# Decoder trunk on one core: the merge gates and branch projections with activations as the stationary operand

## The chip, the cores and the metric

The kernel runs on one core of a Trainium2 chip. The metric is the device time of one launch in microseconds. Three runs of the kernel before gave 1503.16, 1503.56 and 1505.4 us; the median is 1503.56 us. A profile of one execution is shown as rows: engines are PE (TensorE matmul), PEld (TensorE weight load), DVE (VectorE), ACT (ScalarE), POOL (GpSimd) and SP (SyncE, which issues nearly all DMAs here).

## The reference

One layer of a decoder trunk for 256 tokens of width 2048. The part around the change:

```python
proj = h @ w_in                       # columns: q, kv, gates, mLSTM inputs, merge_g (2 x 2048)
y_nsa = nsa_attention(...)            # 256 x 1024
y_ml = mlstm(...)                     # 256 x 1024
g_nsa, g_ml = split(sigmoid(merge_g))
merged = g_nsa * (y_nsa @ w_br_nsa) + g_ml * (y_ml @ w_br_ml)     # 256 x 2048
y = merged @ w_o
```

Before it stand a modulated layer norm and the first 5664 columns of the input projection, after it a residual with two layer norms, a gated MLP with a depthwise convolution (w_up, w_down), and a last norm. The modulation vectors (shift, scale, gate, twice) are a matrix-vector product of a conditioning vector with w_ada, 50 MB of weights.

## The kernel before

**Precision and tiles.** A product is made of three fp32r matmuls: each operand is split into a high part and a rest, and high x high, high x rest and rest x high are summed in PSUM. `load_split` (L99 to L111) streams one 512 KB weight tile (128 x 1024) by SP's queue into one of seven `w` buffers, ACT rounds it into `wh` (L109, four buffers) and DVE subtracts to get `wl` (L110, four buffers).

**Which operand stands still.** A matmul loads a 128 x 128 stationary operand and streams up to 512 columns of the other. `mm_b` holds 128 weight columns still and streams 256 tokens (three matmuls of 256 columns); the result has channels on the partitions. `mm_a` holds 128 tokens of the activations still and streams 512 weight columns (three matmuls of 512 columns for each half of the tokens); the result has tokens on the partitions. The down and output projections (`proj_rows`) and the blocks `ps_a` of the input projection use `mm_a`; the merge gates (tile `ps_mg`) and the branch projections (`ps_br`) use `mm_b`.

**Stages.** The input projection runs over four groups of k tiles (`GROUPS` = 3, 4, 5, 4 of 128 rows); each group does 24 blocks `ps_b`, then 6 blocks `ps_a` in two halves. In the last group the mLSTM gates are worked out as well (`gate_steps`: cumulated forget gates, tile `ps_F`; the compressed-attention scores, `ps_sc`; a transposition `ps_uT`; a running maximum by a scan on DVE, L477; the way back, `ps_mc`, L481; its negative `nT4`, L484 and L485). Then comes the attention and mLSTM stage, in an order on PE that is written out by hand: between its short, dependent pieces (`ml_weights` with `ps_w` and `ps_S`, `nsa_probs`, `nsa_out`, `ml_out`) a call `fill(n)` puts n weight tiles of the merge gates, 40 tiles in all. The merge stage does the other merge gates and all branch projections, multiplies, adds and splits the result into `mgT` (channels on the partitions), the operand of the output projection `ps_o`. Outside the stage with the hand-written order, a scheduler sets the order on each engine.

**The second stream.** The w_ada products run on DVE (L182, tile `w` times the row `crow`, one 512 KB tile each, through the same seven `w` buffers). A ticker hands them out at a rate per weight tile: a share worked out from the group sizes in the first three groups, `GR1` in the last, and the three `RATES`: while filling, in the merge stage, in the output projection. What is left by tile 22 of the output projection is put in at once (`tk.drain`).

**PSUM.** Two pools of four banks: `psm` for the big products, `psa` for the rest.

Of the kernel before, what the change touches and what calls it, by code (L numbers as in the profile page):

```python
# [14 lines left out]
P = 128  # L15
# [38 lines left out]
def build(ctx: ExitStack, tc: tile.TileContext, d, out, dbg=None):  # L54
# [280 lines left out]
    gates0 = pg.tile([P, NG0, 512], F32, name="gates0", tag="gates0")  # L335
# [98 lines left out]
    def gate_steps(misc):  # L434
# [3 lines left out]
        nc.scalar.activation(gsig, projA[:, :, A_G:A_G + 24], AF.Sigmoid)  # L438
        nc.scalar.activation(so, so, AF.Sigmoid)
# [6 lines left out]
        nc.vector.tensor_sub(lf, mn, lf)  # L446
        yield
# [51 lines left out]
    for gi, kn in enumerate(GROUPS):  # L499
        nxt = gi < len(GROUPS) - 1  # L500
        if nxt:
            tk.add(ada_mod(k0 + kn, k0 + kn + GROUPS[gi + 1]))
            rate = 4 * GROUPS[gi + 1] / (6 * kn)
        else:
            rate = GR1
# [27 lines left out]
        for c in range(6):  # L533
            pss = [bank(psm, "ps_a%d" % t) for t in range(2)]
            aw = AW if c < 4 else 512
            for k in range(k0, k0 + kn):
                wh, wl = next(wa if c < 4 else wv)
                for t in range(2):
                    mm_a(pss[t][:, :aw], hT, k, t, wh, wl, k == k0, k == k0 + kn - 1)
                if not nxt and c > 2 and (k - k0) % 2:  # L540
                    next(steps, None)
            for t in range(2):
                dst, src = projA[:, t, c * AW:(c + 1) * AW], pss[t][:, :aw]
                if c >= 4:
                    dst = mv1[:, t, 2 * c - 8:2 * c - 6, :MDV]
                    src = src.rearrange("p (h v) -> p h v", v=MDV)
                if gi == 0:
                    nc.scalar.copy(dst, src)
                else:
                    nc.vector.tensor_add(dst, src, dst)  # L550
            if not nxt:
                if c == 2:
                    while comp:
                        work()
                    misc = pa.tile([P, 4, S], F32, name="misc", tag="c4")
                    steps = gate_steps(misc)
                    next(steps)
# [3 lines left out]
    for _ in steps:  # L561
        pass
# [25 lines left out]
    def paired_gen(w, i0, kt, xt, nm):  # L588

        ps = bank(psm, "ps_" + nm)  # L590
        for b in range(2):
            for hf in range(kt):
                wh, wl = load_split(w[i0 + b * kt + hf])
                for k in range(8):
                    mm_b(ps[:, b * S:(b + 1) * S], wh, wl, k, xt[b], hf * 8 + k, hf == 0 and k == 0,
                         hf == kt - 1 and k == 7)
                yield
        yield ps

    def paired(w, i0, kt, xt, rate, nm):  # L600
        for ps in paired_gen(w, i0, kt, xt, nm):
            if ps is None:
                tk.tick(rate)
        return ps

    def merge_pair(j, rate):
        return paired(d["w_mg"], j * 4, 2, (hT, hT), rate, "mg")
# [3 lines left out]
    def fill_gen():  # L611
        for j in range(NG0 + NG1):
            for ps in paired_gen(d["w_mg"], j * 4, 2, (hT, hT), "mg"):
                if ps is None:
                    yield
            if j < NG0:
                nc.scalar.copy(gates0[:, j, :], ps)
            else:
                held[j] = ps
# [175 lines left out]
    with tc.manual_schedule(engines={mybir.EngineType.PE}):  # L795
        fill(F0)
# [26 lines left out]
        fill(4 * (NG0 + NG1))  # L823
# [11 lines left out]
    nc.scalar.activation(gates0, gates0, AF.Sigmoid)  # L835
    for j in MORD:
        if j < NG0:
            gt = gates0[:, j, :]
        else:
            gt = t2([P, 512], "gt")  # L840
            nc.scalar.activation(gt, held.pop(j) if j in held else merge_pair(j, RATES[1]), AF.Sigmoid)
# [102 lines left out]
    def hold_o(c, k, m):  # L944
        if c == 0 and k < KD // 2:
# [5 lines left out]
                     ((4, load_x), (12, lambda: load_ln(lnr, 0)), (22, tk.drain)))  # L951
# [202 lines left out]
def pack(inputs):  # L1154
# [87 lines left out]
```

## Time and profile before

| | us |
|---|---|
| median of 3 runs | 1503.56 |
| the profiled execution | 1502.99 |
| its span, first to last instruction | 1501.1 |
| PE busy | 1447.9 |
| DVE busy | 1104.9 |
| ACT busy | 726.6 |

The stages in that execution, from the span's start: start and input projection to 308 us, attention with filling to 480, merge to 641, output projection to 726, norms to 758, MLP to 1484, last norm to 1501.1. A matmul's row gives its own duration, which is longer than the distance to the next one, since matmuls overlap; the rate is read from the starts, or from a row of the chain that has many of them (its time over its count). The granted clock is a share of 2.4 GHz: 1.00 or 0.50 (1.2 GHz).

### The profile page before, as it was taken

The page shows a single profiled execution, that of the slowest core. Times are in us where ns is not written, and L with a number is a line of the kernel's source. Part 1 is how long each engine was busy: PE and PEld are TensorE (multiplying, and loading weights), DVE is VectorE, ACT ScalarE, POOL GpSimd, SP SyncE. Part 2 cuts the span into 40 slices and gives each one's busy share as a digit, 9 for nine tenths or more (in the row PEclk, how much of TensorE's full clock was granted, in tenths as well). Part 3 has the DMA queues.
Part 4 walks back from the last instruction along what each step waited for, and adds up shares of the span by engine and source line. Part 5 has one row for each costly group of instructions (what it writes and reads, how often), then busy time and mean ns, then how long its engine had stood idle before and what let it go on. Part 6 is the DMA issues. An engine that isn't in the chain of part 4 may idle for free.

```text
span 1501.1 us, 23706 instructions
## 1 busy us (share of the span) xinstructions
PE 1447.9 (96%) x9178; PEld 1298.6 (87%) x9178; DVE 1104.9 (74%) x1669; ACT 726.6 (48%) x1037; POOL 2.1 (0%) x6
## 2 busy tenths in 40 slices
PE   5999999989999999999699999999999999999997
PEld 4989998879889999988688888888898888888887
DVE  7889886777776888778878878865556666665566
ACT  5644343637555444434465554553335555554341
POOL 0000000000000000000000000000000000000000
PEclk7999999989999999999799999999999999999998
DMA  9999897865768999898368868866666666666661
GB/s 360 349 332 360 287 321 277 295 220 171 286 204 274 339 344 340 291 365 321 111 212 279 281 229 285 271 209 196 193 190 195 191 186 191 187 188 190 196 209 59
DMA packets 103792, 374.84 MB, mean 250 GB/s; under 512 B 11648, under 2 KB 11776, under 8 KB 102912
## 3 DMA queue, kind: packets, MB, share of 16 engines
q1 hardware_dynamic: 103680, 373.34, 73.6%
q8 instruction: 72, 1.18, 0.3%
q14 instruction: 40, 0.33, 0.1%
HBM read 371.19 MB, written 2.10 MB: 249 GB/s over the span
## 4 chain that ended last, share of the span: by engine, by line
PE 86%; DVE 8%; DMA 3%; issue 2%; ACT 1%; SPq 0%; DVEq 0%; ACTq 0%
PE ps_up L83 33%; PE ps_d L83 16%; PE ps_mg L83 12%; PE ps_b L83 7%; PE ps_br L83 6%; PE ps_o L83 4%; PE ps_a L83 4%; DVE w L182 2%; DVE wl L110 2%; PE ps_y L83 1%; ACT wh L109 1%; PE ps_s L83 1%; DVE xz L937 1%; DVE xz L932 1%; DMA xt<-in_x_dram 1%
## 5 line engine op out<-in xcount | busy, mean ns | idle before, releaser
L110 DVE TENSOR_TENSOR wl<-w,wh 128x1024 fp32r<-128x1024 f32 (+1 forms) x478 | 575.6, 1206 | 331.9 <-ACT wh L109 328.4
L109 ACT CAST wh<-w 128x1024 fp32r<-128x1024 f32 (+1 forms) x478 | 495.5, 1038 | 659.0 <-PE ps_up L83 150.3
L83 PE MATMUL ps_up<-h2T,wh 128*128 128x512 f32 x1408 | 496.4, 396 | 0.0
L83 PE MATMUL ps_up<-h2T,wl 128*128 128x256 f32 x1408 | 396.2, 282 | 0.0
L83 PEld LDWEIGHTS ps_up<-h2T,wh 128*128 128x128 f32 x1408 | 265.4, 189 | 62.2
L83 PEld LDWEIGHTS ps_up<-h2T,wl 128*128 128x128 f32 x1408 | 264.7, 188 | 0.1
L182 DVE SCALAR_TENSOR_TENSOR w<-w,crow 128x1024 f32<-128x1024 f32 x192 | 232.7, 1217 | 0.0
L83 PE MATMUL ps_d<-wh,uTt 128*128 128x512 f32 (+1 forms) x792 | 210.6, 354 | 0.0
L83 PE MATMUL ps_mg<-hT,wh 128*128 128x256 f32 x1024 | 188.9, 286 | 0.0
L83 PEld LDWEIGHTS ps_mg<-hT,wh 128*128 128x128 f32 x1024 | 158.0, 188 | 7.2 <-issue 7.0
L83 PEld LDWEIGHTS ps_d<-wh,uTt 128*128 128x128 f32 x792 | 140.4, 189 | 20.6
L83 PE MATMUL ps_b<-hT,wh 128*128 128x256 f32 x768 | 138.3, 283 | 5.4 <-ACT wh L109 4.0
L83 PE MATMUL ps_mg<-hT,wl 128*128 128x256 f32 x512 | 143.1, 280 | 0.0
L83 PE MATMUL ps_d<-wl,uTt 128*128 128x512 f32 (+1 forms) x396 | 140.0, 354 | 0.0
L83 PEld LDWEIGHTS ps_b<-hT,wh 128*128 128x128 f32 x768 | 118.6, 191 | 10.3 <-ACT wh L109 4.8
L83 PE MATMUL ps_a<-wh,hT 128*128 128x392 f32 (+1 forms) x384 | 110.6, 364 | 0.0
L83 PE MATMUL ps_b<-hT,wl 128*128 128x256 f32 x384 | 106.7, 282 | 1.3 <-DVE wl L110 1.3
L83 PEld LDWEIGHTS ps_mg<-hT,wl 128*128 128x128 f32 x512 | 96.4, 188 | 0.0
L83 PEld LDWEIGHTS ps_d<-wl,uTt 128*128 128x128 f32 x396 | 74.9, 189 | 10.4
L83 PEld LDWEIGHTS ps_a<-wh,hT 128*128 128x128 f32 x384 | 71.6, 190 | 8.2 <-issue 2.1
L83 PEld LDWEIGHTS ps_b<-hT,wl 128*128 128x128 f32 x384 | 72.6, 190 | 3.0 <-DVE wl L110 2.2
L83 PE MATMUL ps_a<-wl,hT 128*128 128x392 f32 (+1 forms) x192 | 69.5, 362 | 0.0
(248 smaller groups left out, 1390.7 us busy)
## 6 DMA issues: line engine op xcount, KB each, us to landing
w<-in_w_ada_dram SPq DMA_DIRECT2D x192, 512.0 KB, 4.9
w<-in_w_up_dram SPq DMA_DIRECT2D x176, 512.0 KB, 4.4
w<-in_w_down_dram SPq DMA_DIRECT2D x90, 512.0 KB, 4.1
w<-in_w_mg_dram SPq DMA_DIRECT2D x64, 512.0 KB, 5.0
w<-in_w_in_b_dram SPq DMA_DIRECT2D x48, 512.0 KB, 5.3
w<-in_w_br_dram SPq DMA_DIRECT2D x32, 512.0 KB, 5.1
w<-in_w_o_dram SPq DMA_DIRECT2D x32, 512.0 KB, 5.5
w<-in_w_in_a_dram SPq DMA_DIRECT2D x32, 392.0 KB, 4.6
```

What stands on the lines that cost most here:

```text
L83: nc.tensor.matmul(o, lhsT, rhs, start=start, stop=stop)
L109: nc.scalar.copy(wh[:, :n], t[:, :n])
L110: lows.append(nc.vector.tensor_sub(wl[:, :n], t[:, :n], wh[:, :n]))
L182: ins = nc.vector.scalar_tensor_tensor(t, t, 1.0, crow[:, i * 1024:(i + 1) * 1024], op0=ALU.mult, op1=ALU.mult, accum_out=parts[:, m, k, i ...
L932: nc.vector.scalar_tensor_tensor(z, z, mv[:, 0:1], lg[:, c * 512:(c + 1) * 512], op0=ALU.subtract, op1=ALU.mult)
L937: nc.vector.scalar_tensor_tensor(z, z, mv[:, 2:3], lb[:, c * 512:(c + 1) * 512], op0=ALU.mult, op1=ALU.add, accum_out=acc)
```

## The change

Merge gates and branches are done with `mm_a`: 512 weight columns stream past stationary activations, and a unit of 512 gate channels takes two banks of `psm` (one per half of the tokens) and 8 weight tiles (4 for a branch). The weights are packed to match. The multiplied and added blocks have tokens on the partitions, so `turn_merged` turns them by 32 transpositions on TensorE into `mgT`; the last of these stand behind the second tile of the output projection. The sum over both branches is taken before the turn. Filling keeps 40 tiles (5 units of 8), of which four now stand ahead of the first `ml_weights`, where one stood. In `gate_steps` the cumulated gates come ahead of the compressed scores, and the steps are spread over two blocks of `ps_a` and the first filling. The ticker's rates, the number of warm-up matmuls and the share of the first groups change.

```diff
-RATES = (0.8, 0.85, 0.3)
+RATES = (1.0, 0.7, 0.55)
-NG0, NG1 = 8, 2
-WARM = 16
-F0 = 1
-MORD = (8, 9, 0, 1, 10, 2, 11, 3, 12, 4, 13, 5, 14, 6, 15, 7)
+NU0, NU1 = 4, 1
+WARM = 20
+MORD = (0, 2, 1, 3)
...
-            rate = 4 * GROUPS[gi + 1] / (6 * kn)
+            rate = 4 * GROUPS[gi + 1] / (6 * kn - 2)
...
-                if not nxt and c > 2 and (k - k0) % 2:
-                    next(steps, None)
+                if not nxt and c in (3, 4) and (k - k0) % 2:
+                    next(steps)
...
-    def paired_gen(w, i0, kt, xt, nm):
-
-        ps = bank(psm, "ps_" + nm)
-        for b in range(2):
-            for hf in range(kt):
-                wh, wl = load_split(w[i0 + b * kt + hf])
-                for k in range(8):
-                    mm_b(ps[:, b * S:(b + 1) * S], wh, wl, k, xt[b], hf * 8 + k, hf == 0 and k == 0,
-                         hf == kt - 1 and k == 7)
-                yield
-        yield ps
...
+    def rows_gen(w, i0, tiles, xT, nm):
+
+        pss = [bank(psm, "ps_%s%d" % (nm, t)) for t in range(2)]
+        for i in range(tiles):
+            wh, wl = load_split(w[i0 + i])
+            for j in range(2):
+                k = 2 * i + j
+                for t in range(2):
+                    mm_a(pss[t], xT, k, t, wh[:, j * 512:(j + 1) * 512], wl[:, j * 512:(j + 1) * 512],
+                         k == 0, k == 2 * tiles - 1)
+            yield
+        yield pss
...
-        fill(F0)
+        fill(2)
+        for _ in steps:
+            pass
+        fill(2)
...
-        tmp = t2([P, 512], "mt")
-        ps = paired(d["w_br"], j * 2, 1, (y_nsaT, y_mlT), RATES[1], "br")
-        nc.vector.tensor_mul(tmp, ps, gt)
-        nc.vector.tensor_add(tmp[:, :S], tmp[:, :S], tmp[:, S:])
-        nc.scalar.copy(mgT[:, j, 0, :], tmp[:, :S])
-        nc.vector.tensor_sub(mgT[:, j, 1, :], tmp[:, :S], mgT[:, j, 0, :])
+
+    def turn_merged(c, tmps):
+        for t in range(2):
+            ps = bank(psa, "ps_mT")
+            for i in range(4):
+                nc.tensor.transpose(ps[:, i * P:(i + 1) * P], tmps[t][:, i * P:(i + 1) * P], ident)
+            src = ps.rearrange("p (i s) -> p i s", i=4)
+            hi, lo = [mgT[:, 4 * c:4 * c + 4, h, t * P:(t + 1) * P] for h in range(2)]
+            nc.scalar.copy(hi, src)
+            nc.vector.tensor_sub(lo, src, hi)
...
+            pss = rows(d["w_br"], u * 4, 4, yT, RATES[1], "br")
+            for t in range(2):
+                nc.vector.tensor_mul(gt[t], pss[t], gt[t])
+            if turn_late:
+                turn_late()
...
+        for t in range(2):
+            nc.vector.tensor_add(both[0][t], both[0][t], both[1][t])
+        turn_late = lambda c=c, tmps=both[0]: turn_merged(c, tmps)
...
-                     ((4, load_x), (12, lambda: load_ln(lnr, 0)), (22, tk.drain)))
+                     ((2, turn_late), (4, load_x), (12, lambda: load_ln(lnr, 0)), (22, tk.drain)))
```

On PE in the merge stage, before: the end of a block of merge gates and the start of its branch, weights stationary (named last), 256 columns out.

```order
L83 MATMUL ps_mg<-hT,wh 128x256 x2
L83 MATMUL ps_mg<-hT,wl 128x256
L83 MATMUL ps_br<-y_nsaT,wh 128x256 x2
L83 MATMUL ps_br<-y_nsaT,wl 128x256
L83 MATMUL ps_br<-y_nsaT,wh 128x256 x2
```

Now, at the end of the second branch unit over `y_mlT`:

```order
L82 MATMUL ps_br_4916<-wh,y_mlT 128x512
L82 MATMUL ps_br_4916<-wl,y_mlT 128x512
L82 MATMUL ps_br_4916<-wh,y_mlT 128x512
L839 MATMUL ps_mT<-cst,gates_205 128x128 x8
L82 MATMUL ps_br_5012<-wh,y_nsaT 128x512
L82 MATMUL ps_br_5012<-wl,y_nsaT 128x512
L82 MATMUL ps_br_5012<-wh,y_nsaT 128x512
```

Each matmul is twice as wide and there are half as many; eight transpositions of the block before stand between two units.

On PE at the seam of input projection and attention, before: the last matmuls of the one filled tile, then the two transpositions `ps_mc`, which read what the scan wrote, and at once the first `ml_weights`, which reads `nT4` (both in tile `misc`).

```order
L83 MATMUL ps_mg<-hT,wh 128x256 x2
L83 MATMUL ps_mg<-hT,wl 128x256
L481 MATMUL ps_mc<-cst,misc 128x4 x2
L83 MATMUL ps_w<-misc,cst 128x384
L83 MATMUL ps_w<-identr,maskr 128x2x128
L83 MATMUL ps_S<-accM 128x256
```

Now, at the same place; 38 matmuls of the filling stand between `ps_uT` and the first row here:

```order
L480 MATMUL ps_mc<-cst,misc 128x4 x2
L82 MATMUL ps_mg_3254<-wh,hT 128x512
L82 MATMUL ps_mg_3255<-wh,hT 128x512
L82 MATMUL ps_mg_3255<-wl,hT 128x512
L82 MATMUL ps_mg_3255<-wh,hT 128x512
L82 MATMUL ps_mg_3254<-wh,hT 128x512
L82 MATMUL ps_mg_3254<-wl,hT 128x512
L82 MATMUL ps_mg_3254<-wh,hT 128x512
L82 MATMUL ps_mg_3255<-wh,hT 128x512
L82 MATMUL ps_mg_3255<-wl,hT 128x512
L82 MATMUL ps_mg_3255<-wh,hT 128x512
L82 MATMUL ps_w<-misc,cst 128x384
```

Before, 24 matmuls of 256 columns and two pieces of `ps_a` stood between `ps_uT` and `ps_mc` and none between `ps_mc` and `ps_w`; now it is 38 of 512, and then ten.

On DVE at that seam, before: one weight tile's rest (`wl`) and one w_ada product, the copy of the transposed gates, two additions to `projA`, the scan (written `misc<-uT`), and `nT4` (L484, L485).

```order
L110 TENSOR_TENSOR wl<-w,wh 128x1024
L182 SCALAR_TENSOR_TENSOR w,parts<-w,crow 128x1024
L476 COPY uT<-ps_uT 4x256
L550 TENSOR_TENSOR projA<-ps_a_3198,projA 128x2x256
L550 TENSOR_TENSOR projA<-ps_a_3199,projA 128x2x256
L477 SCALAR_TENSOR_TENSOR misc<-uT 4x256
L110 TENSOR_TENSOR wl<-w,wh 128x1024
L182 SCALAR_TENSOR_TENSOR w,parts<-w,crow 128x1024
L484 TENSOR_SCALAR misc<-misc 4x256
L485 TENSOR_SCALAR misc<-misc 4x128
L482 TENSOR_TENSOR sm<-sm,ps_mc 128x8
```

Now:

```order
L109 TENSOR_TENSOR wl<-w,wh 128x1024
L181 SCALAR_TENSOR_TENSOR w,parts<-w,crow 128x1024
L549 TENSOR_TENSOR projA<-ps_a_3202,projA 128x2x256
L549 TENSOR_TENSOR projA<-ps_a_3203,projA 128x2x256
L475 COPY uT<-ps_uT 4x256
L109 TENSOR_TENSOR wl<-w,wh 128x1024
L181 SCALAR_TENSOR_TENSOR w,parts<-w,crow 128x1024
L476 SCALAR_TENSOR_TENSOR misc<-uT 4x256
L109 TENSOR_TENSOR wl<-w,wh 128x1024
L181 SCALAR_TENSOR_TENSOR w,parts<-w,crow 128x1024
L483 TENSOR_SCALAR misc<-misc 4x256
L484 TENSOR_SCALAR misc<-misc 4x128
```

One more pair of tile rest and product stands between the copy and the scan. Ahead of these rows, from the moment the scores are in PSUM, the order now has one more tile rest and one more product too, and one addition to `projA` less.

On DVE in the output projection, before: what `tk.drain` put behind the second block's statistics.

```order
L872 BN_STATS st_0_6971<-xz 128x6 x2
L872 BN_STATS st_1_6972<-xz 128x6 x2
L110 TENSOR_TENSOR wl<-w,wh 128x1024
L182 SCALAR_TENSOR_TENSOR w,parts<-w,crow 128x1024 x7
L110 TENSOR_TENSOR wl<-w,wh 128x1024 x2
```

Now, at the same statistics:

```order
L902 BN_STATS st_0_5816<-xz 128x6 x2
L902 BN_STATS st_1_5817<-xz 128x6 x2
L109 TENSOR_TENSOR wl<-w,wh 128x1024
L181 SCALAR_TENSOR_TENSOR w,parts<-w,crow 128x1024 x2
L109 TENSOR_TENSOR wl<-w,wh 128x1024 x2
```

Seven products in a row became two; the other five stand one by one further up.

## Rows read from the trace of the kernel before

**Rows 1.** The page's first part: busy us, share of the span, instructions.

```profile
PE 1447.9 (96%) x9178; PEld 1298.6 (87%) x9178; DVE 1104.9 (74%) x1669; ACT 726.6 (48%) x1037; POOL 2.1 (0%) x6
```

**Rows 2.** Windows, one row per stage: first two groups of the input projection (two rows), attention, merge, output projection. Columns: us, busy time of PE, PEld, DVE, ACT, POOL (instructions), granted clock, busy share of the DMA engines, GB/s.

```profile
32.00:80.00 48.00, 47.81 (x323) 45.85 (x322) 39.63 (x55) 30.17 (x46) 0.00 (x0) 0.97 0.97 357
80.00:152.00 72.00, 67.39 (x456) 63.45 (x456) 68.34 (x104) 31.53 (x37) 0.00 (x0) 0.98 0.96 343
...
321.00:466.00 145.00, 143.43 (x1023) 126.06 (x1022) 99.12 (x182) 86.37 (x177) 0.00 (x0) 1.00 0.64 217
480.00:641.00 161.00, 161.00 (x1353) 160.91 (x1353) 137.04 (x195) 68.60 (x81) 0.00 (x0) 1.00 0.92 328
641.00:726.00 85.00, 83.64 (x445) 72.12 (x444) 69.19 (x101) 36.89 (x38) 0.00 (x0) 1.00 0.93 340
```

**Rows 3.** The chain of work that ended last, in order of time: start us, us, what, how many.

```profile
316.75 2.12 PE ps_w L83 x3
318.87 1.28 PE ps_S L83 x4
320.15 3.44 PE ps_mg L83 x24
323.59 1.15 PE ps_w L83 x3
325.39 2.83 PE ps_mg L83 x24
...
502.76 11.30 PE ps_mg L83 x96
514.06 11.52 PE ps_br L83 x96
...
628.16 0.87 PE ps_adar L215 x8
...
640.55 40.83 PE ps_o L83 x180
```

**Rows 4.** Weight tiles of merge gates and branches, from the page's DMA issues: how many, KB each, us to landing.

```profile
w<-in_w_mg_dram SPq DMA_DIRECT2D x64, 512.0 KB, 5.0
...
w<-in_w_br_dram SPq DMA_DIRECT2D x32, 512.0 KB, 5.1
```

**Rows 5.** Timeline of PE: 512-column matmuls of `ps_a` with `hT` stationary, the first and the last of 18 in a row (17 distances). Columns: start us, us, engine, line, operation, tiles, stationary size, result.

```profile
290.65 0.39 PE L83 MATMUL ps_a<-wh,hT 128*128 128x512 f32 x1
...
294.61 0.40 PE L83 MATMUL ps_a<-wh,hT 128*128 128x512 f32 x1
```

**Rows 6.** Timeline of PE: transpositions at the start, while the granted clock was 0.5, and the first matmuls of the input projection with the idle time before them in brackets.

```profile
20.10 5.38 PE L301 MATMUL ps_nT<-cst,xt 128*128 128x128 f32 x28 [1.54 <-ACT xt L294]
...
31.07 1.07 PE L83 MATMUL ps_b<-hT,wh 128*128 128x256 f32 x4 [1.91 <-ACT wh L109]
```

**Rows 7.** Groups of DVE and ACT in the merge stage: shapes, count, busy us and mean ns, idle us before them and who ended it.

```profile
L110 DVE TENSOR_TENSOR wl<-w,wh 128x1024 fp32r<-128x1024 f32 x56 | 68.5, 1222 | 23.3 <-ACT wh L109 23.0
...
L847 DVE TENSOR_TENSOR mgT<-mt,mgT 128x256 fp32r<-128x256 f32 x15 | 6.3, 419 | 0.0
...
L844 DVE TENSOR_TENSOR mt<-ps_br,gt 128x512 f32<-128x512 f32 x8 | 5.5, 684 | 0.0
...
L109 ACT CAST wh<-w 128x1024 fp32r<-128x1024 f32 x57 | 59.9, 1052 | 93.2 <-PE ps_br L83 42.5 <-PE ps_mg L83 36.4 <-issue 10.7
```

**Rows 8.** Timeline of PE at the seam of input projection and attention; in brackets the idle time before a row and who ended it.

```profile
295.92 3.75 PE L83 MATMUL ps_sc<-kcT,accQ 128*128 128x16 f32 x32
...
308.31 0.40 PE L83 MATMUL ps_mg<-hT,wh 128*128 128x256 f32 x2
...
314.15 0.26 PE L481 MATMUL ps_mc<-cst,misc 4*128 4x4 f32 x2 [2.85 <-DVE misc L477]
316.75 1.61 PE L83 MATMUL ps_w<-misc,cst 4*128 4x384 f32 x2 [2.35 <-DVE sm L482]
```

**Rows 9.** Windows around the seam, columns as in rows 2: the two stretches with a granted clock of 0.50.

```profile
300.90:304.30 3.40, 3.40 (x9) 2.68 (x9) 3.40 (x6) 2.33 (x2) 0.00 (x0) 0.50 0.86 245
...
314.60:321.40 6.80, 4.65 (x14) 3.43 (x15) 4.91 (x10) 0.94 (x3) 0.00 (x0) 0.50 0.73 251
```

**Rows 10.** Timeline of DVE at the seam: the scores taken from PSUM, a tile's rest, a product, the scan, `nT4`.

```profile
305.16 0.41 DVE L453 TENSOR_TENSOR misc<-ps_sc,cst 128x256 f32<-128x256 f32 x1
...
313.33 0.67 DVE L477 TENSOR_TENSOR_SCAN misc<-uT 4x256 f32<-4x256 f32 x1
313.93 1.19 DVE L110 TENSOR_TENSOR wl<-w,wh 128x1024 fp32r<-128x1024 f32 x1
315.05 1.21 DVE L182 SCALAR_TENSOR_TENSOR w<-w,crow 128x1024 f32<-128x1024 f32 x1
...
316.19 0.28 DVE L484 TENSOR_SCALAR misc<-misc 4x256 f32<-4x256 f32 x1
```

**Rows 11.** Who waited on PE in the stretch 226 to 726 us (us in total, times, longest): the row of the output projection.

```profile
PE ps_o L83 <- ACT wh L109: 1.4, 1, 1.4
```

**Rows 12.** A piece of the chain in the output projection (start us, us, what).

```profile
695.44 5.58 DMA w<-in_w_o_dram
```

**Rows 13.** Timeline of PE at the start of the second group of the input projection, rows with idle time before them.

```profile
80.70 0.50 PE L83 MATMUL ps_b<-hT,wh 128*128 128x256 f32 x2 [0.69 <-ACT wh L109]
...
84.09 1.02 PE L83 MATMUL ps_b<-hT,wh 128*128 128x256 f32 x4 [1.40 <-ACT wh L109]
```

More of the change, by code (lines that the diff above doesn't have):

```diff
@@ L332, in build @@
     run_all(ada_mod(0, GROUPS[0]))
-    gates0 = pg.tile([P, NG0, 512], F32, name="gates0", tag="gates0")
+    gates0 = pg.tile([P, NU0, 2, 512], F32, name="gates0", tag="gates0")
     ast = ExitStack()
@@ L446, in gate_steps @@
         nc.vector.tensor_sub(lf, mn, lf)
+        nc.scalar.activation(gsig, projA[:, :, A_G:A_G + 24], AF.Sigmoid)
+        nc.scalar.activation(so, so, AF.Sigmoid)
+        yield
+        ps = bank(psa, "ps_F")
+        mm(ps[:, 0:4], upper, lf[:, 0, :], True, True)
+        mm(ps[:, 4:8], ones, lf[:, 0, :], True, False)
+        mm(ps[:, 4:8], upper, lf[:, 1, :], False, True)
+        nc.vector.tensor_copy(fc, ps[:, :8].rearrange("p (a b) -> p a b", a=2))
+        nc.vector.tensor_sub(uc, gif[:, :, 0:4], fc)
         yield
@@ L560, in build @@
             tk.drain()
-    for _ in steps:
-        pass
     dump("hT", hT.bitcast(F32))
@@ L586, in narrow, with rows @@
             nc.vector.tensor_add(dst[:, b * S:(b + 1) * S], ps[:, :S], dst[:, b * S:(b + 1) * S])
[L588 to L602 removed]
+    def rows_gen(w, i0, tiles, xT, nm):
[7 more added lines that the diff above has]
+                         k == 0, k == 2 * tiles - 1)
+            yield
+        yield pss
+    def rows(w, i0, tiles, xT, rate, nm):
+        for pss in rows_gen(w, i0, tiles, xT, nm):
+            if pss is None:
                 tk.tick(rate)
[L604 to L607 removed]
+        return pss
     held = {}
     def fill_gen():
[L612 to L614 removed]
+        for u in range(NU0 + NU1):
+            for pss in rows_gen(d["w_mg"], u * 8, 8, hT, "mg"):
+                if pss is None:
                     yield
[L616 to L617 removed]
+            if u < NU0:
+                for t in range(2):
+                    nc.scalar.copy(gates0[:, u, t, :], pss[t])
             else:
[L619 removed]
+                held[u] = pss
     filler = fill_gen()
@@ L822, in build @@
         outs(1, 1)
-        fill(4 * (NG0 + NG1))
+        fill(8 * (NU0 + NU1))
     dump("y_nsaT", y_nsaT.bitcast(F32))
@@ L834, in build, with sigmoids, gate_tiles @@
     mgT = pm.tile([P, KD, 2, S], F32R, name="mgT")
[L835 to L841, printed above, removed]
-        tmp = t2([P, 512], "mt")
-        ps = paired(d["w_br"], j * 2, 1, (y_nsaT, y_mlT), RATES[1], "br")
-        nc.vector.tensor_mul(tmp, ps, gt)
-        nc.vector.tensor_add(tmp[:, :S], tmp[:, :S], tmp[:, S:])
-        nc.scalar.copy(mgT[:, j, 0, :], tmp[:, :S])
-        nc.vector.tensor_sub(mgT[:, j, 1, :], tmp[:, :S], mgT[:, j, 0, :])
+    def turn_merged(c, tmps):
[7 more added lines that the diff above has]
+            nc.vector.tensor_sub(lo, src, hi)
+    def sigmoids(dst, src):
+        for t in range(2):
+            nc.scalar.activation(dst[t], src[t], AF.Sigmoid)
+        return dst
+    def gate_tiles():
+        return [pm.tile([P, 512], F32, name="gt", tag="gt", bufs=6) for _ in range(2)]
+    for u in held:
+        held[u] = sigmoids(gate_tiles(), held[u])
+    turn_late = None
+    for c in MORD:
+        both = []
+        for kind, yT in ((1, y_mlT), (0, y_nsaT)):
+            u = 2 * c + kind
+            if u < NU0:
+                gt = [gates0[:, u, t, :] for t in range(2)]
+                sigmoids(gt, gt)
+            elif u in held:
+                gt = held[u]
+            else:
+                gt = gate_tiles()
+                sigmoids(gt, rows(d["w_mg"], u * 8, 8, hT, RATES[1], "mg"))
+            pss = rows(d["w_br"], u * 4, 4, yT, RATES[1], "br")
+            for t in range(2):
+                nc.vector.tensor_mul(gt[t], pss[t], gt[t])
+            if turn_late:
+                turn_late()
+                turn_late = None
+            both.append(gt)
+        for t in range(2):
+            nc.vector.tensor_add(both[0][t], both[0][t], both[1][t])
+        turn_late = lambda c=c, tmps=both[0]: turn_merged(c, tmps)
     dump("mgT", mgT.bitcast(F32))
```

16 lines of the change are left out of this document (4 added, 12 removed).

## The prediction

> **What bounds the kernel now.** I read the first part of the page first: PE is busy for 96% of the span [rows 1], so time is gained only by fewer PE nanoseconds or by closing PE's gaps. Next the windows by stage [rows 2]: in the attention, merge and output-projection windows PE is busy for 143.4 of 145, all of 161 and 83.6 of 85 us, while DVE has room in the first (99.1 of 145) and less in the second (137.0 of 161). Only the first two groups of the input projection are bound elsewhere: the DMA engines are 96 to 97% busy there. Then the chain [rows 3]: through the merge it is nothing but long runs of `ps_mg` and `ps_br` matmuls, which give the real distance between two matmuls. Last come the timelines at the places where the chain leaves PE: the seam to the attention [rows 8], the output projection [rows 11] and the second group [rows 13].
>
> **The matmuls.** There are 64 tiles of merge gates and 32 of branches [rows 4], 24 matmuls of 256 columns each: 1536 and 768. At 11.30/96 = 117.7 ns and 11.52/96 = 120.0 ns [rows 3] they take 180.8 + 92.2 = 273.0 us. The change streams the same number of columns by 768 + 384 matmuls of 512. The trace has two distances for those: 40.83/180 = 226.8 ns in `ps_o`, with `mgT` stationary [rows 3], and 3.96/17 = 232.9 ns in `ps_a`, with `hT` stationary [rows 5]. The merge gates have exactly the operands of `ps_a`, so I take 232.9 for them: 178.9 us. No row has a branch in this form; I take the middle, 229.9: 88.3 us. The sum is 267.2, a gain of **5.8 us**; with 226.8 everywhere it is 11.7, with 232.9 everywhere 4.7.
>
> **The turns.** 32 transpositions are new on PE. At full clock eight (`ps_adar`) take 0.87 us [rows 3], so 32 cost **+3.5 us**; at half clock 5.38/28 = 192 ns each [rows 6], 6.1 us, is the other end. They don't wait for DVE: the order puts the first three turns behind a later branch unit of 48 matmuls (some 11 us), and the last behind two tiles of the output projection (24 x 227 ns = 5.4 us), ahead of which DVE has two multiplications and two additions of 0.68 us [rows 7] and a tile's rest or two.
>
> The Trainium skill has prices for both (TensorE: Matmul & The Clock Gate, sections Back-to-back issue gap and Part 4: PE-mode transpose): a gap of N/2.4 + 2.5 ns, 109 and 216 ns here, and some 275 ns for a transposition. By these the matmuls would gain 3.0 us and the turns cost 8.8. The rows disagree with both.
>
> **DVE and ACT in the merge.** Before, each of 16 blocks costs DVE 0.684 + 2 x 0.42 us [rows 7], 24.3 us; now 16 multiplications, 8 additions and 8 subtractions of 512 columns, 32 x 0.684 = 21.9 us. Also the rate falls from 0.85 to 0.7, on 56 tiles 8 products fewer. All of it lies beside PE and is worth nothing by itself: DVE already idles 23.3 us there, waiting for ACT, which waits for PE to free `wh` [rows 7].
>
> **The seam.** PE stands for 2.85 us before `ps_mc`, which waits for the scan, and 2.35 us before the first `ps_w`, which waits for `nT4` [rows 8]: 5.2 us. What is late next? DVE. From the scores to the end of the scan it needs 314.0 - 305.16 = 8.8 us [rows 10]. The new order adds to this stretch a tile's rest and two products (3 x 1.15 us) and an uncovered exponential (about 0.5, an estimate from the 0.42 us rows around it), and takes no time off, since the moved `projA` addition now stands ahead of it: the scan ends near 317.9. PE reaches `ps_mc` after 38 matmuls of 232.9 ns, at 308.3 + 8.85 = 317.2: a wait of 0.7. `nT4` follows one rest and one product later (2.3 us, then 0.5), near 320.7; PE has ten matmuls (2.3 us) and waits 0.3. With 0.2 for `ps_uT`, 1.2 of the 5.2 us stay. Behind the waiting matmuls stands the rest of the filling, so a wait there is paid in full.
> The granted clock is 0.50 from 314.6 to 321.4 [rows 9], after those two waits. The first `ml_weights` with its filled tile takes 2.12 + 1.28 + 3.44 = 6.84 us, the second, at full clock, 325.39 - 323.59 + 2.83 = 4.63 [rows 3]; so the low clock costs 2.2 us, and with PE nearly always busy it should not fall. The earlier fall, at 300.9, follows 3.75 us of 16-column `ps_sc` matmuls [rows 8], which stay. Together **-6.2 us**; ends -7.4 (no wait left) and 0 (the wait only moves).
>
> **The output projection.** PE waits 1.4 us [rows 11], behind the seven products in a row and the weights that landed late because their buffers were held [rows 12]. At 0.55 a tile most of these are done before: **-1.4 us**; ends -1.4 and 0.
>
> **The first groups.** The faster share finishes the w_ada products two tiles earlier, so the modulated input of the second group is ready sooner. PE's two largest gaps there are 0.69 and 1.40 us [rows 13]. But the DMA engines set the pace, and no byte is saved: at the first window's 357 GB/s instead of 343 [rows 2] the second would be 72 x 14/357 = 2.8 us shorter. On the other side two weight tiles come later, at 0.524 MB and 357 GB/s 2.9 us. I take **-1 us**. Four more warm-up matmuls (4 x 0.23 us) lie in PE's 1.91 us of waiting for the first weights [rows 6] and cost nothing; without that cover they cost 0.9.
>
> **The filling.** 40 tiles at 1.0 instead of 0.8 put 8 more products on DVE in the attention stage, 8 x 1.30 = 10.4 us; DVE goes from 99.1 to 109.5 of 145 us [rows 2], 76%. PE's dependent pieces have filled tiles ahead of them, so little should show: **+1 us**; ends 0 and +10.4.
>
> **Sum.** -5.8 + 3.5 - 6.2 - 1.4 - 1 + 1 = -9.9 us against the profiled execution's 1502.99. That execution lies 0.57 us below the median of the runs, so the same difference from 1503.56 gives **1493.7 us**. All good ends together give -19.8 (1483.8), all bad ones +14.7, far less likely at once.
>
> **The rivals.**
> *Wide matmuls at the quick distance.* If 226.8 ns holds everywhere, the sum is -15.8: 1487.8 us. For it: `ps_o` keeps it over 180 matmuls. Against: `ps_a`, with the same stationary tile, doesn't. Chance 0.22.
> *The wait at the seam only moves.* If DVE is later than I counted, all 5.2 us and the low clock stay: -3.7, 1499.9 us. For it: at 300.9 to 304.3 DVE had no break at all [rows 9]. Chance 0.16.
> *Slower: DVE sets the pace while filling.* Each of the 8 further products stands ahead of the softmax's reductions in DVE's order; if they all reach PE (10.4 instead of 1) and DVE is late at the seam too (6.2 lost), the sum is +5.7: 1509.3 us. It decides from about 9 us of new PE gaps between 321 and 466 us on. Against it stand the 46 us that DVE idles there [rows 2]. Chance 0.10.
> *Columns alone cost time.* Then half as many matmuls gain nothing, and the turns at the half-clock price take 6.1: -9.9 + 5.8 + 2.6 = -1.5, 1502.1 us. Against it: 117.7 x 2 is more than either wide distance [rows 3, 5]. Chance 0.06. This is where the Trainium skill's section on the issue gap points, with its nearly constant price per column; the trace doesn't agree.
> That leaves 0.46 for the forecast.
>
> **Chances and range.** A measurement of this kernel tells 0.2%, 3.0 us, from no change. Faster than 1500.5: nearly all of the forecast (0.44), the first rival (0.22), a bit over half of the second (0.10): 0.76. Slower than 1506.6: the third (0.10) and a little of the forecast: 0.11. The same: 0.13. The range, 1484 to 1504 us, goes from all good ends to just above no change; it leaves out the slower rival and little else.
>
> **What would show it.** Right: 1152 matmuls `ps_mg` and `ps_br` of 512 columns, at 227 to 233 ns; eight `ps_mT` in about 0.9 us, with no idle time before them; at most 1 us before `ps_mc` and before `ps_w`, and a granted clock of 1.00 from 314 us to the norms; no wait in the output projection. Wrong: distances above 235 ns, PE waiting for `wl` or DVE in the attention stage, a first `ml_weights` that still waits 2 us, or a second group that starts later than 79.6 us.

## The result and the profile after

The changed kernel takes 1495.19 us (median of 4 runs, 1492.45 to 1495.93), the kernel before beside it 1503.36 us (1502.01 to 1505.4). The ratio is 0.9941, with a 95% interval of 0.9924 to 0.9958: faster by about 8.2 us, where 9.9 were forecast. The profiled execution, 1492.45 us with a span of 1490.3, is the quickest of the four, so the two traces lie 10.8 us apart (span 1501.1 before), 2.6 more than the medians.

The page's first part, answering to [rows 1], and the granted clock in its 40 slices:

```profile
PE 1443.5 (97%) x8062; PEld 1239.3 (83%) x8062; DVE 1103.0 (74%) x1653; ACT 734.1 (49%) x1042; POOL 2.1 (0%) x6
...
PEclk9999999999999999999899999999999999999999
```

The windows by stage, answering to [rows 2] with the same columns. The last two windows begin 14 and 15 us earlier than before, the stages themselves less: the merge's first branch at 472.6 us instead of 479.7, the first `ps_o` at 631.3 instead of 640.4.

```profile
32.00:80.00 48.00, 46.70 (x317) 43.45 (x316) 40.45 (x56) 31.13 (x47) 0.00 (x0) 1.00 0.99 368
80.00:152.00 72.00, 69.99 (x499) 66.68 (x498) 68.12 (x104) 32.35 (x39) 0.00 (x0) 1.00 0.96 349
...
305.00:321.00 16.00, 16.00 (x71) 12.21 (x69) 15.97 (x28) 6.36 (x9) 0.00 (x0) 1.00 0.82 287
321.00:466.00 145.00, 140.04 (x604) 102.91 (x604) 106.72 (x199) 94.47 (x189) 0.00 (x0) 1.00 0.71 250
466.00:626.00 160.00, 160.00 (x705) 129.53 (x705) 124.64 (x158) 67.12 (x73) 0.00 (x0) 1.00 0.88 311
626.00:712.00 86.00, 86.00 (x444) 73.66 (x443) 72.61 (x98) 39.42 (x40) 0.00 (x0) 1.00 0.92 335
```

Read the first and second number of a row against each other. In the second group PE is idle for 2.0 us instead of 4.6, though in the first for 1.3 instead of 0.2; at the seam (305 to 321) not at all, with the clock at 1.00; in the output projection not at all. In the attention it went the other way: 5.0 us idle instead of 1.6.

The chain in order of time (start us, us, what, how many), answering to [rows 3]:

```profile
305.24 8.87 PE ps_mg L82 x38
...
314.32 2.54 PE ps_mg L82 x10
316.85 1.15 PE ps_w L82 x3
...
472.64 21.67 PE ps_br L82 x94
494.31 22.40 PE ps_mg L82 x96
516.71 11.24 PE ps_br L82 x48
527.95 0.87 PE ps_mT L839 x8
...
551.83 10.93 PE ps_br L82 x48
...
640.73 55.36 PE ps_o L82 x244
```

`ps_mg` comes every 22.40/96 = 233.3 ns, `ps_br` every 234.2 with `y_mlT` stationary (11.24/48) and 227.7 with `y_nsaT` (10.93/48), eight turns take 0.87 us, and no piece stands between them. The first `ps_w` takes 1.15 us where it took 2.12.

Four moments of PE place the difference, here for all kernels that were run (us from the span's start, each from one profiled execution): the end of the last `ps_a`, the first `ps_o`, the first `ps_up`, the end of PE's last matmul. The last column is the median of the timed runs, with the median of the runs of the kernel before on the same chip.

| kernel | ps_a ends | ps_o | ps_up | PE ends | us (before) |
|---|---|---|---|---|---|
| before | 308.5 | 640.4 | 747.1 | 1490.2 | 1503.36 |
| changed | 305.0 | 631.3 | 736.9 | 1479.3 | 1495.19 (1503.36) |
| turned_only | 310.5 | 639.7 | 749.6 | 1492.9 | 1506.46 (1502.76) |
| rates_before | 306.9 | 632.3 | 740.1 | 1482.1 | 1495.13 (1502.76) |
| seam_before | 307.1 | 644.6 | 750.3 | 1492.8 | 1506.04 (1502.76) |
| share_before | 308.3 | 634.5 | 740.2 | 1482.5 | 1499.87 (1502.76) |
| all_but_turned | 306.3 | 639.1 | 744.2 | 1486.9 | 1499.74 (1502.08) |
| one_sigmoid | 307.1 | 637.1 | 742.7 | 1484.6 | 1498.86 (1502.08) |
| fill_sigmoid | 306.0 | 632.1 | 737.7 | 1478.6 | 1493.62 (1502.08) |
| weights_low | 309.0 | 637.3 | 744.9 | 1487.8 | 1499.62 (1502.08) |
| aligned | 310.7 | 635.0 | 740.7 | 1487.7 | 1496.69 (1501.89) |
| before_aligned | 310.2 | 641.6 | 748.4 | 1490.8 | 1511.17 (1501.89) |
| aligned_fill | 309.5 | 630.8 | 736.5 | 1483.1 | 1496.33 (1501.89) |
| placed_fill | 308.4 | 631.9 | 737.5 | 1474.9 | 1488.07 (1502.67) |

Of the traces' 10.9 us, 3.5 come before the end of `ps_a`, 5.6 from there to the output projection, 1.1 in that and the norms and 0.7 in the MLP.

The runs of one kernel spread over up to 9 us, so a difference below some 2 us between two medians is not read as one here, and a single trace shows where time can go, not how often it goes there. Differences to the changed kernel are between the medians as they stand; the kernel before moved by 1.5 us from one set of runs to the next.

### The profile page after: what moved, and what is told of

It is laid out like the page before. It is cut to its first block, busy times and chain, and to the rows that moved or that the text cites. A ratio compares the mean times of both kernels' runs of the same rounds, so it can differ in the third digit from the quotient of the medians.

```text
span 1490.3 us, 21477 instructions
## 1 busy us (share of the span) xinstructions
PE 1443.5 (97%) x8062; PEld 1239.3 (83%) x8062; DVE 1103.0 (74%) x1653; ACT 734.1 (49%) x1042; POOL 2.1 (0%) x6
## 4 chain that ended last, share of the span: by engine, by line
PE 86%; DVE 7%; DMA 3%; ACT 2%; issue 2%; SPq 0%; DVEq 0%; ACTq 0%
PE ps_up L82 33%; PE ps_d L82 16%; PE ps_mg L82 11%; PE ps_br L82 6%; PE ps_a L82 6%; PE ps_o L82 5%; PE ps_b L82 5%; DVE w L181 2%; DVE wl L109 1%; DMA w<-in_w_in_b_dram 1%; PE ps_y L82 1%; ACT wh L108 1%; DVE xz L962 1%; DVE xz L967 1%; PE ps_hid L82 1%
## 5 line engine op out<-in xcount | busy, mean ns | idle before, releaser
L108 ACT CAST wh<-w 128x1024 fp32r<-128x1024 f32 (+1 forms) x478 | 495.6, 1038 | 640.4 <-PE ps_up L82 150.6
L82 PE MATMUL ps_mg<-wh,hT 128*128 128x512 f32 x512 | 172.4, 408 | 0.0
L82 PEld LDWEIGHTS ps_mg<-wh,hT 128*128 128x128 f32 x512 | 96.2, 188 | 26.0 <-issue 4.1
L82 PE MATMUL ps_mg<-wl,hT 128*128 128x512 f32 x256 | 101.1, 395 | 0.0
L82 PE MATMUL ps_o<-wh,mgT 128*128 128x512 f32 (+1 forms) x224 | 65.1, 374 | 0.0
```

Of the source, the lines that this page charges most:

```text
L82: nc.tensor.matmul(o, lhsT, rhs, start=start, stop=stop)
L108: nc.scalar.copy(wh[:, :n], t[:, :n])
```

## The experiments

### One part alone, or one part undone

**turned_only**: `RATES`, `WARM`, the share, the gate chain and the filling's start of the kernel before; the new merge stays.

> The kernel before with nothing but the new merge: gates and branches in 512 columns, merged blocks turned on PE; rates, gate chain, filling start, share and warm-up are those of before. My theory: the matmuls give 5.1 to 5.8 us and the turns take 3.5, so 1.6 to 2.3 us faster than before; the waits before ps_mc and ps_w and the half clock behind them stay (5.2 and 2.2 us). Rival 1, columns alone cost time: no gain, 2 to 3 us slower. Rival 2, the gate sigmoids that ACT now runs one by one load their table in the attention stage and hold PE there: new PE waits of 2 to 4 us between 321 and 466 us, so 0 to 2 us slower than before.

Measured: ratio 1.0028 (1.0015 to 1.004), 3.7 us slower than before. Who waited on PE (us in total, times, longest) from 309 to 480 us, and the windows of low clock:

```profile
PE ps_y L82 <- ACT pT L634: 3.2, 3, 2.1
PE ps_w L82 <- DVE misc L484: 2.3, 1, 2.3
```

```profile
300.30:307.10 6.80, 6.80 (x19) 5.47 (x19) 6.80 (x15) 2.75 (x3) 0.00 (x0) 0.50 0.86 286
317.30:320.80 3.50, 3.50 (x11) 2.85 (x11) 1.74 (x4) 0.73 (x2) 0.00 (x0) 0.51 0.76 252
703.10:706.50 3.40, 3.32 (x9) 2.75 (x10) 3.36 (x6) 2.79 (x4) 0.00 (x0) 0.50 1.03 417
```

No theory had that. In the trace it is 2.7 us shorter than before from `ps_a` to `ps_o` (329.2 against 331.9), about what was expected of the matmuls. It is lost around that: `ps_a` ends 2.0 us later, with falls of the clock at 82 and at 300 us that last some 6.8 us each instead of 3.4, and output projection and norms take 3.2 us longer, with a wait of 1.8 us and a fall behind it. So the merge's gain is there where it is made, and too small to survive such losses; why they came with the merge is not shown. Rival 2 saw the new wait before `ps_y`, but not, as one_sigmoid shows, its cause.

**all_but_turned**, its counterpart: everything but the new merge.

> The kernel before with everything but the new merge: the new gate chain, the new start of the filling, the new share, rates and warm-up; gates and branches stay in 256 columns. Theory of the prediction (the merge itself gives 2.3 us): 2.3 us slower than the changed kernel, some 6 to 8 us faster than before. By turned_only, which was 3.7 us slower than before: the merge costs, and this kernel is about 3 us faster than the changed one. Theory ACT: with one copy a block instead of two together, the 3.1 us wait before ps_y is about 1 us as in the kernel before, so the merge's gain in the matmuls and this loss cancel: within 1 us of the changed kernel, with the attention stage some 2 us shorter and the merge some 2 us longer.

Measured: 0.9982 (0.9972 to 0.9992), 2.3 us faster than before and 4.5 us slower than the changed kernel, more than any theory gave. The waits in its attention stage:

```profile
PE ps_y L83 <- ACT pT L636: 5.0, 3, 2.5
PE ps_s L83 <- DVE y_nsaT L719: 1.0, 1, 1.0
```

The new waits before `ps_y` and `ps_s` are here too, without one instruction of the new merge, and turned_only has the first without the rest of the change: whichever part is made, ACT gets another order. The two halves don't add: 3.7 and -2.3 us alone, -8.2 together. Each half has a wait of about 2 us that the whole doesn't have (before `ps_w` there; here a second one before `ps_y`, near 451 us), and each of these has a stretch of low clock behind it (317.3 to 320.8 us there, 454.1 to 457.5 here). That explains part of it; the rest stays open.

**seam_before**: the sigmoids ahead of the exponentials, `ps_F` behind the scan, `fill(1)` after the steps.

> The changed kernel with the old gate chain, the cumulative sums behind the scan's start, and the old start of the filling. My theory: PE waits again about 2.9 us before ps_mc and 2.4 us before ps_w, and the granted clock is 0.5 for some 6 us behind it: 6 to 7.5 us slower than the changed kernel. Rival 1, the wait went because of the wide matmuls or the earlier scan, not by the order: less than 2 us slower. Rival 2, only the waits count and the low clock comes anyway elsewhere: 5 us slower, with the same sum of time at half clock.

Measured: 1.0029 (1.0018 to 1.004), 10.9 us slower than the changed kernel. Its waits and the windows of low clock:

```profile
PE ps_y L82 <- ACT pT L634: 6.4, 3, 5.2
PE ps_w L82 <- DVE misc L484: 2.3, 1, 2.3
PE ps_mc L480 <- DVE misc L476: 1.4, 1, 1.4
```

```profile
313.10:319.90 6.80, 6.04 (x14) 4.20 (x15) 3.62 (x9) 0.94 (x3) 0.00 (x0) 0.50 0.88 304
374.50:381.40 6.90, 3.67 (x7) 2.26 (x8) 6.90 (x12) 4.60 (x9) 0.00 (x0) 0.51 0.75 254
```

The seam waits come back (3.7 us), the wait before `ps_y` is 3.3 us longer than in the changed kernel, and PE works 6.0 + 3.7 us at half clock, of which half is lost (4.9): 11.9 us, against 11.2 from `ps_a` to `ps_o` in the table. The order of the gate chain was worth more than its own two waits. Rivals 1 and 2 fall.

**share_before**: `6 * kn` for `6 * kn - 2`, 16 warm-up matmuls.

> The changed kernel with the old share of w_ada products in the first groups (6 kn instead of 6 kn - 2 tiles) and 16 warm-up matmuls. My theory of the prediction: 1 us slower than the changed kernel. By the changed kernel's trace, whose last ps_a ends 3.3 us earlier than before: 3.3 us slower. Rival, the third group starts later but its matmuls come at 113.5 instead of 118.1 ns, which gives back half: the third group starts some 7 us later, the fourth some 3.5. Rival, DMA alone sets the pace of both and the difference of the two traces is chance: within 0.7 us of the changed kernel.

Measured: 0.9982 (0.9972 to 0.9993), 4.7 us slower than the changed kernel; `ps_a` ends 3.3 us later in the trace, which is of its quickest run, 1495.57. PE's timeline at the start of the second group, where the changed kernel has no wait (its own, of 1.7 us, comes at 131 us):

```profile
78.89 0.50 PE L82 MATMUL ps_b<-hT,wh 128*128 128x256 f32 x2 [0.69 <-ACT wh L108]
...
82.28 1.02 PE L82 MATMUL ps_b<-hT,wh 128*128 128x256 f32 x4 [1.39 <-ACT wh L108]
```

These are the gaps of [rows 13] again, to 0.01 us, and the clock falls behind them (84.2 to 87.6 us). They and the fall (between 81.8 and 89.3 us) are in the four traces with the old share, and in none of the ten with the new one. So they belong to the share, and not to the bytes that the DMA engines move, which are the same; the 16 warm-up matmuls were undone with it and are not told apart.

**rates_before**: `RATES = (0.8, 0.85, 0.3)`.

> The changed kernel with the old shares of filling work, (0.8, 0.85, 0.3) products a tile. Theory DVE: the 3.1 us that PE waits before ps_y near 372 us and the 1.1 us near 417 us come from the 8 more products on DVE; they go (to about 1 us in sum, as before), and the wait of 1.4 us in the output projection comes back: 1.5 to 2.5 us faster than the changed kernel. Rival ACT: these waits come from the sigmoids and copies of the new units on ACT; they stay within 1 us, and with the wait in the output projection it is 1 to 1.5 us slower than the changed kernel. Rival: the old rates keep both (no wait in the output projection without the old merge): equal within 1 us.

Measured: 0.9958 (0.9945 to 0.9971), 1495.13 us: the same as the changed kernel. Of its waits on PE, one from 309 to 480 us and the one from 626 to 726:

```profile
PE ps_y L82 <- ACT pT L634: 2.0, 1, 2.0
```

```profile
PE ps_o L82 <- ACT wh L108: 1.6, 1, 1.6
```

The wait before `ps_y` falls from 3.1 to 2.0 us, that before `ps_s` stays at 1.1, one of 0.7 us before `ps_n` is new, and the output projection waits 1.6 us for ACT again. Both sides of the rates are there and cancel.

### The wait before ps_y

The changed kernel's waits on PE from 309 to 480 us, and behind them the first of them before; the second was absent there.

```profile
PE ps_y L82 <- ACT pT L634: 3.1, 1, 3.1
PE ps_s L82 <- DVE y_nsaT L717: 1.1, 1, 1.1
PE ps_s L82 <- DVE y_mlT L779: 0.6, 1, 0.6
```

```profile
PE ps_y L83 <- ACT pT L638: 0.9, 1, 0.9
```

The chain there tells why: after PE has turned the probabilities, ACT copies them (`pT`), but has other work first.

```profile
367.15 3.08 ACT num L764 x6
370.23 1.89 ACT wh L108 x2
372.12 1.61 ACT pt L689 x4
373.73 0.95 ACT gates L613 x2
374.68 0.94 ACT wh L108
...
376.16 1.12 PE ps_y L82 x2
```

**one_sigmoid** takes the sigmoids' table loads out of the stage: `nc.scalar.activation(gates0, gates0, AF.Sigmoid)` at the merge's start, and none for each unit.

> The changed kernel with one sigmoid over all of gates0 where the merge starts, as before, instead of pairs that stand in the attention stage on ACT, so 6 table loads less. If the sigmoids and their table loads hold PE in the attention stage: the 3.1 us before ps_y and the 1.1 us before ps_s go, 3 us faster than the changed kernel. If it is ACT's order (eight num, two casts, four pt and two gate copies ahead of the pT copy, 9.3 us): one cast of 0.94 us less stands ahead, so the wait is still about 2.2 us, at most 1 us faster.

Measured: 0.9979 (0.9968 to 0.9989), 3.7 us slower than the changed kernel. The first of its waits from 309 to 480 us:

```profile
PE ps_y L82 <- ACT pT L634: 5.4, 2, 3.2
```

With six table loads less (15 against 21, 1.28 us each) the wait before `ps_y` is still 3.2 us, with a fall of the clock behind it (379.3 to 382.7 us) that the changed kernel's trace doesn't have, and a second one of 2.2 us follows near 453 us, in another place of ACT's order. So the table loads were not the cause, and the scheduler's new order of ACT made a worse one.

**fill_sigmoid**: in addition `fill(4)` for `fill(3)` ahead of `outs(0, 0)`, and of the `fill(2)` behind `probs(1, 1)` one tile ahead of it.

> As one_sigmoid, and one more filled tile on PE before outs(0, 0) and one moved ahead of probs(1, 1), both from behind: the same work in another order. If PE's wait before ps_y is ACT's time (the pT copy ends when it ends), a tile of 12 x 233 ns = 2.8 us fills it: the wait falls from 3.1 to 0 to 0.4 us, that before ps_s from 1.1 to 0, and it is 3 to 4 us faster than the changed kernel. If the tile's own cast on ACT and product on DVE push the copy back, the wait stays and it is within 1 us.

Measured: 0.9947 (0.9933 to 0.996), 1493.62 us: 5.2 us faster than one_sigmoid, by the filled tiles alone.

```profile
PE ps_s L82 <- DVE nm L661: 2.6, 1, 2.6
PE ps_y L82 <- ACT pT L634: 1.3, 1, 1.3
```

The first wait falls to 1.3 us and the one near 453 us goes; the tile moved ahead of `probs(1, 1)` gives a new wait of 2.6 us for DVE. So it was the length of ACT's queue against PE's cover, as the second theory said, but only part of the 3 to 4 us was kept.

### The two distances

The prediction could not say why 512-column matmuls come 227 ns apart with `mgT` and 233 with `hT`. In the changed kernel `y_nsaT` falls to one side and `y_mlT` to the other, in the same loop. In the built program `wh`, `wl`, `mgT`, `uTt` and `y_nsaT` all start at 480 modulo 512 bytes in their partitions, `hT` at 288 and `y_mlT` at 64.

**weights_low**: the pools `p0` and `wp` opened in the other order. `wh` starts at 128 then; the others keep theirs.

> The changed kernel with two pools opened in the other order: the weights w, wh and wl lie at low SBUF addresses, and hT and y_mlT above them. In the trace matmuls of 512 columns come 227 ns apart with mgT, uTt or y_nsaT stationary, which lie above the moving wh, and 233 with hT or y_mlT, which lie below. If where the two operands lie sets the distance: ps_mg and ps_br y_mlT fall to 227 ns, 960 x 6.5 ns = 6 us faster, and ps_a and ps_up perhaps with them. If it is the stage (what else DVE, ACT and the DMA engines do in it): ps_mg stays at 233, equal within 1 us.

Measured: 0.9984 (0.9975 to 0.9993), 4.4 us slower than the changed kernel; of the 8.5 us between the traces 4.0 stand before the end of `ps_a`. Its chain in merge and MLP:

```profile
500.06 22.40 PE ps_mg L82 x96
522.46 10.99 PE ps_br L82 x48
...
557.43 11.24 PE ps_br L82 x48
...
995.72 124.10 PE ps_d L82 x660
```

The two branches have changed places: `y_mlT` 229.0 ns, `y_nsaT` 234.2. `ps_d`, 121.47 us in the kernel before and in the changed one, takes 124.10, and `ps_o` rose to 234 ns. So it is not the stage, and not that the weights lie above or below; the start came into question.

**aligned**: `hT`, `h2T` and `y_mlT` start at 480 too, by the order in which the small tiles `epsc`, `modc`, `cs` and `parts` are allocated.

> The changed kernel, its small tiles allocated in another order so that hT, h2T and y_mlT start at the same place modulo 512 bytes as wh, wl, mgT and y_nsaT; not an instruction's work differs. In the changed kernel 512-column matmuls come 226.8 ns apart where both operands start alike (mgT, uTt, y_nsaT with wh) and 233 to 234 where not (hT, y_mlT); in weights_low, where mgT and uTt no longer start like wh, those rose to 234. Theory, the start modulo 512 sets the distance: ps_mg, ps_a and ps_br y_mlT fall to 227 ns (768 x 6.5 + 192 x 7.2 + 192 x 6.5 ns = 7.6 us), 256-column ps_b may rise by 1.7 ns x 1152 = 2 us, ps_up may fall by up to 4.4 ns a pair x 1408 = 6 us: 6 to 12 us faster than the changed kernel. Rival, the distance between the tiles or the bank they lie in sets it: all distances stay within 1 ns, equal within 1.5 us.

Measured: 0.9965 (0.9952 to 0.9978), 1496.69 us: no faster than the changed kernel, where 6 to 12 us were expected. The trace is of its slowest run, 1500.84. Its chain:

```profile
501.02 21.76 PE ps_mg L86 x96
522.78 10.88 PE ps_br L86 x48
...
557.19 10.90 PE ps_br L86 x48
```

All three are at 227 ns: 226.7, 226.7, 227.1. The theory holds for 512 columns; from `ps_a` to `ps_o` it is 2.0 us shorter although PE's clock falls twice more (380.7 to 384.1 and 425.1 to 428.5 us). It does not pay in the whole: the 256-column `ps_b` rises from 116.8 to 119.9 ns (means of 1117 and 1100 distances at full clock, without some 16 near 225 ns, as far as two; 3.6 us over its 1152), and the MLP is 4.6 us longer.

**before_aligned**: the same order in the kernel before.

> The kernel before with the same order of small tiles. Its gates and branches are matmuls of 256 columns, 117.7 and 120 ns apart. If the start modulo 512 matters for the wide form alone: ps_mg goes from 118 to about 120 ns (1536 x 1.7 = 2.6 us slower), ps_a falls to 227 (1.2 us faster), ps_up falls by 0 to 6 us: between 1 us slower and 5 us faster than before; the wide form then gives 2 x 120 - 227 = 13 ns a pair, 15 us over the 1152 wide matmuls of the merge, against 5.8 in the prediction. If it matters for the narrow form in the same measure, ps_mg falls to 114.5 ns and the merge's gain stays 5 to 6 us.

Measured: 1.0051 (1.0033 to 1.0069), 1511.17 us, 9.3 us slower than before, outside both theories; its trace is of its quickest run, 1503.57, so what the others lose isn't seen. Its chain:

```profile
502.71 11.52 PE ps_mg L87 x96
514.23 11.52 PE ps_br L87 x96
```

The narrow `ps_mg` goes from 117.7 to 120.0 ns. What helps the wide form hurts the narrow one: two narrow matmuls against one wide are 240.0 to 226.7 ns here, and 235.4 to 233.3 with `hT` where it was.

**aligned_fill**, aligned and fill_sigmoid together:

> Both together: the order of small tiles of aligned, and the filling of fill_sigmoid (which was 1.4 us faster than the changed kernel). If the two are independent, the gain of aligned and that of fill_sigmoid add: 1482 to 1487 us. If shorter tiles in the filling only lengthen PE's waits for ACT and DVE in the attention stage, 2 to 3 us of it are lost there.

Measured: 0.9955 (0.9939 to 0.9971), 1496.33 us: they don't add. In the traces, from `ps_a` to `ps_o` it is the shortest of all (321.3 us), and all that it has there over fill_sigmoid (326.1) is lost in the input projection and the MLP.

**placed_fill** draws the consequence: fill_sigmoid with `y_mlT` at the start of the weights, and `hT` and `h2T` 160 bytes further, as they stood in weights_low, where the narrow `ps_up` ran best.

> fill_sigmoid with the starts chosen by the earlier runs: y_mlT starts like wh, mgT and uTt modulo 512 bytes, hT and h2T 160 bytes further on, as they stood to wh in weights_low. From the distances measured there: ps_br y_mlT falls from 234 to 227 ns (192 x 7.2 = 1.4 us), ps_up from 231.7 + 119.4 to 229.2 + 117.6 ns a pair (1408 x 4.3 = 6.1 us), ps_mg stays at 233.5, ps_o and ps_d at 227, ps_b rises from 118.3 to 119.7 ns (1152 x 1.4 = 1.6 us): 5 to 6 us faster than fill_sigmoid, 1486 to 1489 us. If the starts are not what sets the distances of ps_up, or the earlier filling of PE makes new waits in the attention stage, within 1.5 us of fill_sigmoid.

Measured: 0.9912 (0.9894 to 0.993), 1488.07 us, 5.6 us faster than fill_sigmoid and some 7 faster than the changed kernel: the quickest that was run.

```profile
518.26 10.92 PE ps_br L85 x48
...
749.45 131.53 PE ps_up L85 x759
...
1109.59 244.06 PE ps_up L85 x1408
```

The changed kernel's `ps_up` pieces are 133.94 us (x759) and 245.62 (x1408). Fill_sigmoid, with the changed kernel's starts, has 132.42 us for the first of these and the same 245.62 for the second. What is open: `ps_up` has the same operands in both halves of the MLP, and 133.94/759 = 176.5 ns in the first against 174.4 in the second; aligned has 176.5 and 176.7, before_aligned 173.3 and 176.7. Only with the 160 bytes, in two kernels, are both at 173.3. So the start isn't all that acts on narrow matmuls.

## Why the prediction was right

The total was right, -8.2 us against -9.9, but in part by luck: the first groups gave 2.5 us more than counted, and the attention stage took back 2.3. The terms, by the two traces:

- **Matmuls, -5.8.** 768 x 233.3 ns and 384 x 230.5 (21.67/94, both branches) are 267.7 us: -5.3. The distance of `ps_a` held for `ps_mg`, since it is the same tile `hT` at the same place, and the middle held for the branches, since one of their tiles starts like the weights and the other doesn't; neither reason was known, so that the middle held is luck. The rival with the quick distance everywhere is what aligned made of it. The Trainium skill (TensorE: Matmul & The Clock Gate, section Back-to-back issue gap) works out the gap from the width alone; these traces have 226.7 to 234.3 ns for 512 columns. (The estimate of 3.0 us that I worked out from its formula comes to 2.9.)
- **Turns, +3.5.** 4 x 0.87 us, no wait before them: exact.
- **Seam, -6.2.** No wait is left and no half clock from 302.7 us on: -7.4, the good end. I let DVE be 0.7 us late, by a count that was too long: from the scores to the end of the scan I had 8.8 + 3.95 = 12.8 us, and it took 10.0 (302.66 to 312.67; in share_before, whose `ps_a` ends at 308.3, 306.22 to 316.23, and no wait either). In this stretch the order had one product more than before and one addition to `projA` less, not a tile's rest and two products more. The rival that the wait only moves is out.
- **Output projection, -1.4.** The wait of 1.4 us is gone, and rates_before brings 1.6 back.
- **First groups, -1.** This step failed. I took the DMA engines as the pace, since they are 96 to 97% busy; the trace gives -3.5 at the end of `ps_a`, and share_before's takes 3.3 of it back. What I priced at nothing were PE's waits for ACT's `wh` at the second group [rows 13], which I had in the rows, and the clock's fall behind them (3.4 us at half clock, 1.7 lost). How much of the 3.5 they are stays open: five other kernels with the new share and the same starts end `ps_a` at 306.0 to 307.1, so that part of it may belong to this one execution, and the waits in the first two groups fell in all only by 1.5 us.
- **Filling, +1.** Mis-sized the other way: waits of 4.8 us instead of 1.5 in the attention stage, so +3.3. But the eight products are little of it: with the old rates (rates_before) 4.4 us of waits are left. What the sum lacked is a term for ACT. I looked at DVE, for which the products are work, and DVE had room; what came late was ACT, whose copy of `pT` stands behind 8.5 us of other work.
- **Not in the sum:** the low clock around the norms lasts from 726.0 to 739.6 us, 3.4 us less than before. That is 0.7 us of the traces' difference, and chance may have made it.

The terms thus measured give -5.3 + 3.5 - 7.4 - 1.4 - 3.5 + 3.3 - 0.7 = -11.5, against 10.9 between the traces. That the medians differ by less is left open: the traced run of the changed kernel is its quickest.

The changed kernel's rows of DVE for the seam, the scores taken from PSUM and the scan:

```profile
302.66 0.41 DVE L459 TENSOR_TENSOR misc<-ps_sc,cst 128x256 f32<-128x256 f32 x1
...
312.00 0.67 DVE L476 TENSOR_TENSOR_SCAN misc<-uT 4x256 f32<-4x256 f32 x1
```

The slower rival, DVE setting the pace, is out: DVE grew by 7.6 us in the attention stage (10.4 were counted), and 3.1 of PE's 4.8 us of waits there are for ACT; the 1.1 us for DVE's `y_nsaT` stays with the old rates. Columns alone cost time: out for 512 columns at the weights' start, nearly true for `hT` where it lies (235.4 to 233.3).

## What to carry to other kernels

Where the same instruction has two distances in one trace, look at where its operands lie before putting it down to the stage: here the start modulo 512 bytes was worth 3% of every wide matmul, and a few small tiles allocated in another order set it. Then measure the whole: much of what the wide matmuls gained in aligned, the narrow ones took back. A wait on the bounding engine has to be priced with the low clock behind it and with the schedule that it shifts; undoing the seam's order cost 11 us for 3.7 us of waits. And parts of a change that each lift a different wait don't add: alone, one half of this one made the kernel slower.

## What the runs showed of the hardware

512-column matmuls at full clock come 226.7 to 227.9 ns apart (means) when the stationary and the moving tile start alike modulo 512 bytes, and 229.0 to 234.3 ns otherwise. For 256 columns there is no such gain, rather the reverse: with alike starts `ps_mg` goes from 117.7 to 120.0 ns and `ps_b` from 116.8 to 119.9, while the narrow branches are at 120.0 either way. Why was not found. The unlike offsets here are 96, 160, 320, 352 and 448 bytes; none is a multiple of 128, so that these runs don't tell a period of 512 bytes from one of 128 or 256. Nor is the start all: with the same starts `ps_b` came every 113.9 ns through 264 matmuls of the changed kernel's second group and every 118.1 through 360 of its third. And of PE's 19 waits of 2 us or more between 36 and 715 us, in all fourteen traces, 12 have a stretch of 3.4 or 6.8 us at half clock with them or behind them, so that half of PE's work there came on top of the wait; behind the changed kernel's own 3.1 us the clock did not fall, behind the same wait in weights_low it did. Near 300 us it fell in every trace without a wait, while the 32 `ps_sc` matmuls of 16 columns ran or up to 1.8 us after them.
